# A hybrid attention layer on one core: a regrouped opening, weight copies and splits in another order, a gate that starts one step later

## The chip, the cores and the metric

One core of a Trainium2 chip runs the whole layer. The time is device microseconds of one execution, the median of three runs. "Before" is the kernel as it was, "after" the kernel with the change.

## The reference, cut to what matters

512 tokens, width 1024, float32, one layer. Group A attends over the 128 best keys that a small indexer picks for each query, group B is latent attention with low-rank queries and keys; both are causal by chunks of 64 tokens.

```python
xn = rms_norm(h, norm_gain[l])
proj = xn @ w_in[l]
(q_a, k_a, v_a, g_a, q_i, k_i, w_i, c_q, c_kv, k_rope, g_b) = jnp.split(proj, offsets, axis=-1)
q_a = rope(rms_norm(q_a), pos); k_a = rope(rms_norm(k_a), pos)      # 8 heads of 64
q_i, k_i = rope(first 32 columns), rest as it is                    # 8 index heads, one index key
o_a = indexer_sparse_attention(q_a, k_a, v_a, q_i, k_i, w_i, pos)   # top 128 keys of 512
q_b = (rms_norm(c_q) @ w_uq); kv = (rms_norm(c_kv) @ w_ukv)         # 384 and 256 wide latents
o_b = chunk_causal_attention(rope/rms q_b, rope/rms k_b, v_b, pos)
mixed = concat([o_a * silu(g_a), o_b * silu(g_b)])
h = h + mixed @ w_out[l]
```

## The kernel before, in words

Every product of two float32 operands is made of three TensorE matmuls on a high and a low half (`mm3`, line 185): high by high, high by low, low by high. The halves are made by a cast on ScalarE and a subtraction: for weights `chunk` (line 266) loads 128 rows into one of three staging tiles `wst` from SP's queue, casts on ScalarE (line 272) to `wh` and subtracts on GpSimd, or VectorE where the plan says "D", (line 275) to `wl`. Weights stand in one plan in the order of their use; `wt` makes a weight at least 8 ahead of its use, and `first` (line 231) orders a ScalarE instruction before the casts of weights that are more than so many ahead. TensorE's order is the order in which the program is written (the weaving of streams by `run`, `take`, `weave`); the other engines are put in order by a scheduler, and `after` adds an order between two instructions of one engine.

**The opening** (lines 202 to 215 and 344 to 504). SP's queue loads four 128-token tiles of x, the identity, three small gain vectors (`grow`) and the weights of the small projection (`k_rope`, `k_i`, `w_i`, 104 columns), then `q_i`'s weights. For each token tile half of the squares are summed on ScalarE and half on VectorE, added on VectorE, raised to -1/2 on GpSimd, and the tile is scaled on VectorE. Then TensorE transposes all four tiles (`x_turn`, 32 transposes); a half is two tiles, and after its second tile ScalarE writes eight high parts `xh` (line 375) and VectorE eight low parts `xl` (line 378). `small_step` (line 487) does the small projection on 256 columns of one half at a time, three matmuls for each of eight row blocks: first half 0 alone, then half 1 with one step of `q_i` after each. `stream` (line 316) interleaves the jobs of one projection: a job is a bank and its row blocks, each job starts some steps after the one before. `q_i` has three query tiles, 8/3 steps apart, and its transposes use the banks "tr". There are eight PSUM banks, named mm (3), tr (2), sc (2) and pv (1), taken in turn.

**Then** come the latent projections `c_kv` and `c_q`, the indexer, top-k passes on VectorE woven through everything, the gates `g_b` (four jobs that start together, banks pv, mm, mm, mm, line 619), the up-projections and attention B, then `g_a`, `q_a`, `k_a`, `v_a`, then attention A with the output projection woven in.

**`proj`** (line 837) handles `q_a` and `k_a`: square on ScalarE, sum on VectorE, `rope_mul` (line 412) into two tiles of the ring `tmp`, their sum at line 847, the scale, and later, in `turn`, four transposes, split, and four copies inside the core (`DUP`, line 834) by SP's queue into the two operand tiles.

**`attention`** (line 694): `qk` scores one head and query tile, adds the mask and takes the minimum on VectorE (line 707), exponentiates on ScalarE (line 709), then for each pair of tiles a reciprocal (line 726) and the normalizing product, on ScalarE (line 732) or GpSimd; `pt` transposes the probabilities in three groups and splits them (line 421); `pv` multiplies by V. `SP` holds the splits of a group, `END` the reciprocal and the products of a pair.

## Time and profile before

| | |
|---|---|
| median of three runs | 341.23 us (340.65 to 341.61) |
| the profiled execution's own time | 340.73 us |
| its span, first to last instruction | 338.9 us |
| TensorE / VectorE / ScalarE / GpSimd busy | 325.3 / 257.5 / 215.5 / 182.7 us |

Busy times of TensorE run from the start of a matmul to the end that is modelled for it; a following matmul starts earlier than that, so a short hole between two starts can hide in a busy TensorE. Idle time of an engine is put down to what ended it. A line such as L127 or L131 is that of a helper (`matmul`, `transpose`), so instructions are told apart by their tiles. Names ending in "q" are an engine's queue: SPq stands for DMA issues.

### The profile page before, as it was taken

The numbers are of one execution on the slowest core, as the hardware profiler recorded it, in microseconds if no ns is written. First come the engines' busy times: TensorE is split into PE (matmuls) and PEld (weight loads), VectorE is DVE, ScalarE is ACT, GpSimd is POOL, SyncE is SP. The second block draws the span as 40 slices with busy tenths as digits, with TensorE's granted clock in tenths as the row PEclk, the third lists the DMA queues.
The fourth block names the chain that finished last, engine by engine and source line by source line (L and its number), as shares of the span: only waits on it lengthen the run. The fifth ranks groups of instructions, "written<-read, shape, count | busy, mean of one in ns | idle before, by whom it ended". The sixth has DMA issues, their size and how long they took to land.

```text
span 338.9 us, 5472 instructions
## 1 busy us (share of the span) xinstructions
PE 325.3 (96%) x1688; PEld 272.1 (80%) x1688; DVE 257.5 (76%) x631; ACT 215.5 (64%) x530; POOL 182.7 (54%) x197
## 2 busy tenths in 40 slices
PE   2899999999999999999999999999999999999995
PEld 2778888887898988888888888888777788788884
DVE  4924679659998496778898989776997667776465
ACT  4935558582656676878877898434326988887210
POOL 1655543365799997135714579538725535647100
PEclk9999999999999999999999999999999999999999
DMA  7753344133024325014200355208877314410006
GB/s 263 202 157 93 110 118 119 60 102 93 22 82 119 96 64 155 1 34 121 69 29 1 88 140 136 74 0 201 220 171 232 102 55 140 126 63 0 2 0 248
DMA packets 28806, 34.83 MB, mean 103 GB/s; under 512 B 5341, under 2 KB 16874, under 8 KB 28778
## 3 DMA queue, kind: packets, MB, share of 16 engines
q1 hardware_dynamic: 28202, 33.57, 35.7%
q10 hardware_dynamic: 576, 0.92, 0.7%
q8 instruction: 13, 0.21, 0.3%
q14 instruction: 15, 0.12, 0.1%
HBM read 27.14 MB, written 2.10 MB: 86 GB/s over the span
## 4 chain that ended last, share of the span: by engine, by line
PE 84%; DVE 5%; ACT 3%; DMA 3%; SPq 2%; issue 1%; POOL 1%; DVEq 0%; ACTq 0%; POOLq 0%
PE mm L127 48%; PE sc L127 12%; PE pv L127 9%; PE tr L131 6%; PE tr L127 5%; PE mm L131 2%; DVE ob L946 2%; ACT xh L375 2%; DMA xin<-in_x 2%; SPq L834 1%; DMA wst<-in_w_in 1%; POOL wl L275 1%; ACT wh L272 1%; PE pv L131 1%; DVE tmp L851 0%
## 5 line engine op out<-in xcount | busy, mean ns | idle before, releaser
L275 POOL TENSOR_TENSOR wl<-wst,wh 128x512 fp32r<-128x512 f32 (+2 forms) x80 | 100.0, 1260 | 52.1 <-ACT wh L272 49.7
L272 ACT CAST wh<-wst 128x512 fp32r<-128x512 f32 (+2 forms) x89 | 51.2, 585 | 29.1 <-DMA wst<-in_w_in 22.0
L127 PE MATMUL mm<-wh,xh 128*128 128x512 f32 x120 | 50.3, 419 | 0.0
L127 PE MATMUL mm<-wl,xh 128*128 128x512 f32 x120 | 47.7, 398 | 0.8 <-POOL wl L275 0.8
L127 PE MATMUL mm<-wh,xl 128*128 128x512 f32 x120 | 47.4, 395 | 0.0
L221 POOL TENSOR_TENSOR sml<-sml,nhalf 128x4 f32<-128x4 f32 (+2 forms) x28 | 31.7, 1136 | 21.8 <-ACT sml L845 13.7
L709 ACT ACTIVATE z<-z,sml 128x256 f32<-128x256 f32 (+2 forms) x64 | 35.9, 561 | 10.4 <-DVE sml L707 9.4
L730 POOL TENSOR_SCALAR z<-z,sml 128x512 f32<-128x512 f32 (+2 forms) x32 | 18.1, 565 | 40.9 <-DVE sml L726 30.9
L127 PE MATMUL mm<-xh,wh 128*128 128x512 f32 x88 | 36.7, 418 | 0.4 <-DVE latl L470 0.4
L127 PE MATMUL mm<-xl,wh 128*128 128x512 f32 x88 | 34.8, 396 | 0.0
L127 PE MATMUL mm<-xh,wl 128*128 128x512 f32 x88 | 34.8, 395 | 0.0
L127 PEld LDWEIGHTS mm<-wh,xl 128*128 128x128 f32 x120 | 22.6, 188 | 5.3
L563 DVE MAX8 m<-acc 128x8 f32<-128x512 f32 (+2 forms) x48 | 26.4, 552 | 0.0
L127 PEld LDWEIGHTS mm<-wl,xh 128*128 128x128 f32 x120 | 22.8, 190 | 4.4 <-POOL wl L275 1.5
L564 DVE MATCH_REPLACE8 acc<-m,acc 128x512 f32<-128x512 f32 (+2 forms) x48 | 26.0, 542 | 0.0
L127 PEld LDWEIGHTS mm<-wh,xh 128*128 128x128 f32 x120 | 22.6, 189 | 3.2 <-issue 0.3
L421 DVE TENSOR_TENSOR pl<-tr,ph 128x512 fp32r<-128x512 f32 (+1 forms) x32 | 17.6, 549 | 5.3 <-ACT ph L421 5.3
L421 ACT CAST ph<-tr 128x512 fp32r<-128x512 f32 (+1 forms) x32 | 15.2, 475 | 8.8 <-PE tr L131 8.5
L707 DVE CUSTOM_DVE_ANT_0 z<-sc,wide,nqb 128x512 f32<-128x512 f32 (+3 forms) x32 | 17.3, 541 | 4.3 <-PE sc L127 4.0
L707 DVE CUSTOM_DVE_ANT_0 z<-sc,acc,nqa 128x512 f32<-128x512 f32 (+2 forms) x24 | 14.6, 610 | 7.3 <-PE sc L127 7.3
L127 PE MATMUL sc<-kl,bhl 96*128 96x512 f32 (+3 forms) x96 | 20.0, 320 | 0.0
L127 PEld LDWEIGHTS mm<-xh,wl 128*128 128x128 f32 x88 | 16.5, 188 | 4.0
(223 smaller groups left out, 863.5 us busy)
## 6 DMA issues: line engine op xcount, KB each, us to landing
wst<-in_w_in SPq DMA_DIRECT2D x48, 256.0 KB, 2.7
wst<-in_w_out SPq DMA_DIRECT2D x16, 256.0 KB, 2.9
xin<-in_x SPq DMA_DIRECT2D x4, 512.0 KB, 4.2
k_a<-tmp SPq DMA_DIRECT2D x16, 128.0 KB, 3.9
ob<-in_x SPq DMA_DIRECT2D x8, 256.0 KB, 4.4
wst<-in_w_in SPq DMA_DIRECT2D x8, 192.0 KB, 2.6
wst<-in_w_uq SPq DMA_DIRECT2D x6, 192.0 KB, 2.4
wst<-in_w_in SPq DMA_DIRECT2D x8, 128.0 KB, 2.2
```

What stands on the lines that cost most here:

```text
L127: nc.tensor.matmul(o, l, r, start=start, stop=stop)
L131: nc.tensor.transpose(o, i, idn)
L221: nc.gpsimd.tensor_tensor(dst, src, nhalf[:, :src.shape[-1]], op=OP.pow)
L272: copies.append(nc.scalar.copy(h, st))
L275: i = E(eng).tensor_tensor(l, st, f32(h), op=OP.subtract)
L375: nc.scalar.activation(h, p, AF.Copy, scale=gains[:, k:k + 1])
L421: return nc.scalar.copy(h, p), nc.vector.tensor_tensor(l, p, f32(h), op=OP.subtract)
L563: nc.vector.max(m, masks[t])
L564: dve[0] = nc.vector.match_replace(masks[t], m, masks[t], -3e38).ins
L707: m = nc.vector.tensor_tensor_reduce(z, sc[:, :n], mask(t), nq(h, t), 3e38, OP.add, OP.min, r[:, i:i + 1])
L709: e = nc.scalar.activation(z, z, AF.Exp, bias=r[:, i:i + 1], scale=-1.0, accum_out=r[:, 2 + i:3 + i])
L730: nc.gpsimd.tensor_scalar(z, z, w, 0.0, op0=OP.mult, op1=OP.add)
```

## The change

The diff with its core kept. In the opening:

- ScalarE starts with a one-element square (`wake`) and then issues the three `grow` loads itself; SP's queue has x, the identity and the small weights.
- Eleven matmuls on a zero tile (`WARM`) are first on TensorE.
- Tile 2 is squared by ScalarE alone; the two sums are added on GpSimd; tile 3 is scaled on GpSimd in two passes.
- TensorE's order is: tile 0, the gains' transpose, tiles 1 and 2, the small projection on row blocks 0 to 3 of half 0, tile 3, row blocks 4 to 7, then half 1 with steps of `q_i`. The matmuls with the low part of the small weight come last, eight of 512 columns; that part is subtracted on VectorE instead of GpSimd.
- `q_i`'s query tiles start 1.99 steps apart, each step with the low weight last (`mm3w`); banks mm, mm, pv; the transposes of two of the three use the banks "sc". `c_kv` takes mm and pv instead of pv and mm.
- `chain` fixes the order of the opening's instructions on ScalarE, VectorE and GpSimd.

Later: the four jobs of `g_b` start 0.35 steps apart, which puts the second step of the first job ahead of the fourth job's first. For `k_a` the product of `rope_mul` stays in PSUM, and two of its four `DUP` copies are issued by ScalarE. In attention A, head 1's exponentials for tiles 2 and 3 come after the products of head 0's last pair, and its passes of line 707 after the reciprocal; a head's exponential for tile 0 comes after the first split of the head before; splits come ahead of the casts of weights more than four ahead.

```diff
+    def mm3w(o, lh, ll, rh, rl, first, last):
+        matmul(o, lh, rh, first, False)
+        matmul(o, ll, rh, False, False)
+        matmul(o, lh, rl, False, last)
...
     for t in range(NT):
         nc.sync.dma_start(xin[t // 2][:, t % 2], xv[:, t])
-        if t == NT - 1:
-            for a in range(0, 8, 4):
-                ks = slice(a, a + 4)
-                nc.sync.dma_start(wst[:, ks, 0:32], wv[:, ks, 3272:3304])
-                nc.sync.dma_start(wst[:, ks, 32:104], wv[:, ks, 2560:2632])
-                nc.scalar.copy(SWH[:, ks], wst[:, ks])
-                nc.gpsimd.tensor_tensor(SWL[:, ks], wst[:, ks], f32(SWH[:, ks]), op=OP.subtract)
         if t == 1:
             nc.sync.dma_start(ident, cst[:, 768:896])
-            nc.sync.dma_start(grow[0:8], norm_gain.rearrange("(k p) -> k p", p=128))
...
+    for a in range(0, 8, 4):
+        ks = slice(a, a + 4)
+        nc.sync.dma_start(wst[:, ks, 0:32], wv[:, ks, 3272:3304])
+        nc.sync.dma_start(wst[:, ks, 32:104], wv[:, ks, 2560:2632])
...
+    zero = sb("pt2", (128, 512), name="zero")
+    nc.vector.memset(zero, 0.0)
+    warm = psum("tr")
+    for _ in range(WARM):
+        matmul(warm, zero[:, 0:128].bitcast(F32R), zero.bitcast(F32R), True, True)
+
+    wake = P.tile([128, 1], F32, name="wake")
+    wake_ = nc.scalar.activation(wake, epsc, AF.Square)
+    for d in (nc.scalar.dma_start(grow[0:8], norm_gain.rearrange("(k p) -> k p", p=128)),
+              nc.scalar.dma_start(grow[8:11], b_q_latent.rearrange("(k p) -> k p", p=128)),
+              nc.scalar.dma_start(grow[11:13], b_kv_latent.rearrange("(k p) -> k p", p=128))):
+        after(d, wake_)
...
+        if t == 2:
+            SQ[t] = nc.scalar.activation(big, xt, AF.Square, scale=D ** -0.5, accum_out=r[:, 0:1])
+            other = epsc
...
+        POW[t] = nc.gpsimd.tensor_tensor(r[:, 2:3], r[:, 0:1], other, op=OP.add), rsqrt(r[:, 3:4], r[:, 2:3])
+        SCL[t] = []
+        for xs in (xt[:, 0:512], xt[:, 512:]) if t in (0, 3) else (xt,):
+            e = nc.gpsimd if t == 3 else nc.vector
...
-            xb[hf] = [psum(b) for b in (("tr", "tr", "sc", "sc"), ("mm", "mm", "mm", "tr"))[hf]]
+            xb[hf] = [psum(b) for b in (("mm", "mm", "mm", "pv"), ("tr", "tr", "sc", "sc"))[hf]]
...
-    for t in range(NT):
-        x_turn(t)
-    sm_acc = psum("pv")
+    x_turn(0)
+    gp = psum("sc")
+    transpose(gp[:, :13], grow[:13], ident[:13, :13])
+    gains_ = nc.scalar.copy(gains, gp[:, :13])
+    x_turn(1)
+    x_turn(2)
+    sm_acc = psum("mm")
     def small_step(hf, k):
         c = slice(hf * 256, hf * 256 + 256)
-        mm3(sm_acc[:104, c], SWH[:, k], SWL[:, k], xh(k)[:, c], xl(k)[:, c], k == 0, k == 7)
+        matmul(sm_acc[:104, c], SWH[:, k], xh(k)[:, c], hf == 0 and k == 0, False)
+        matmul(sm_acc[:104, c], SWH[:, k], xl(k)[:, c], False, False)
...
+    for k in range(4):
+        small_step(0, k)
+    x_turn(3)
+    for k in range(4, 8):
+        small_step(0, k)
+    for a in range(0, 8, 4):
+        ks = slice(a, a + 4)
+        SWD.append(nc.vector.tensor_tensor(SWL[:, ks], wst[:, ks], f32(SWH[:, ks]), op=OP.subtract))
+    qi_ = stream(tok_jobs("q_i", 8, xh, xl, 512, [1, 2, 3], lambda t, a: use_qi(t, a), mm3=mm3w), 3, ("mm", "mm", "pv"), 1.99)
+    for i, ks in enumerate(((0,), (1,), (2, 3), (4, 5), (6, 7))):
+        for k in ks:
+            small_step(1, k)
+        run(take(qi_, i // 2 + 1))
+        if i == 0:
+            xa, xd = [[f[hf, k] for hf in range(2) for k in range(8)] for f in (XA, XD)]
+            chain(wake_, SQ[0], SQ[1], SQ[2], gains_, SQ[3], *xa[:2], SWA[0], *xa[2:4], SWA[1], *xa[4:8], copies[0],
+                  *xa[8:10], copies[1], *xa[10:12], copies[2], *xa[12:], copies[3], copies[4])
+            chain(TTR[0], TTR[1], *SCL[0], *SCL[1], TTR[3], *SCL[2], *xd, dsubs[0], *SWD)
+            chain(*POW[0], *POW[1], *POW[2], *POW[3], *SCL[3], *subs[:3])
...
     for k in range(8):
-        small_step(0, k)
...
+        matmul(sm_acc[:104], SWL[:, k], xh(k), False, k == 7)
...
-            p = psum("tr")
+            p = psum("tr" if t == 1 else "sc")
...
-    lkv = stream(feat_jobs("c_kv", 8, xh, xl, [(0, 128), (128, 128)], lat_kv), 2, ("pv", "mm"), 3)
+    lkv = stream(feat_jobs("c_kv", 8, xh, xl, [(0, 128), (128, 128)], lat_kv), 2, ("mm", "pv"), 3)
...
-    gb_ = stream(gate_jobs("g_b", gB), 4, ("pv", "mm", "mm", "mm"), False)
+    gb_ = stream(gate_jobs("g_b", gB), 4, ("pv", "mm", "mm", "mm"), 0.35)
...
-            if not turn and t == 3:
-                if h == 1:
+            if not turn and h == 1 and t >= 2:
+                after(e, END[0][1])
+                if t == 2:
                     after(m, END[0][0])
-                    after(e, END[0][1])
-                elif h > 1:
-                    after(m, SP[h - 2, 0][1])
+                    after(ZM[h, 3], m)
+            elif not turn and h > 1 and t == 3:
+                after(m, SP[h - 2, 0][1])
+            if not turn and h and t == 0:
+                after(e, SP[h - 1, 0][0])
...
             SP[h, b] = split(ph, pl, p[:, :n])
+            if not turn:
+                first(SP[h, b][0], KEEP_EXP)
...
-            rope_mul(q, m, a3, tab, t, 8, 64)
+            c = q if name == "q_a" else a3
+            rope_mul(c, m, a3, tab, t, 8, 64)
...
-                    DUP(a, h3[HALF[u]])
-                    DUP(b, (l3 if name == "q_a" else h3)[HALF[u]])
+                    if name == "q_a":
+                        DUP(a, h3[HALF[u]])
+                        DUP(b, l3[HALF[u]])
+                    else:
+                        DUP(a, h3[HALF[u]], nc.scalar if u else nc.sync)
+                        DUP(b, h3[HALF[u]], nc.scalar if u else nc.sync)
```

## Rows read from the trace of the kernel before

**Rows 1.** The page's part 1: busy us, share of the span, instructions of each engine.
```profile
PE 325.3 (96%) x1688; PEld 272.1 (80%) x1688; DVE 257.5 (76%) x631; ACT 215.5 (64%) x530; POOL 182.7 (54%) x197
```
**Rows 2.** Waits of TensorE from 20 us on: us in total, times, longest us.
```profile
PE mm L127 <- POOL wl L275: 0.8, 2, 0.5
PE tr L131 <- ACT z L732: 0.6, 1, 0.6
PE pv L127 <- DVE pl L421: 0.4, 1, 0.4
PE mm L127 <- DVE latl L470: 0.4, 1, 0.4
```
**Rows 3.** Timeline of the opening, SP's queue: start us, us, instruction, tiles, count.
```profile
3.10 0.83 SPq L203 DMA_DIRECT2D xin<-in_x  x2
...
16.10 18.68 SPq L268 DMA_DIRECT2D wst<-in_w_in  x13
```
**Rows 4.** The same timeline, ScalarE: the fourth square and two first casts.
```profile
9.13 0.63 ACT L348 ACTIVATE tmp<-xin 128x512 f32<-128x512 f32 x1 [1.00 <-DMA xin<-in_x]
...
9.77 1.19 ACT L375 ACTIVATE xh<-tr,gains 128x256 fp32r<-128x256 f32 x3
...
14.01 0.89 ACT L375 ACTIVATE xh<-mm,gains 128x256 fp32r<-128x256 f32 x2
```
**Rows 5.** The same timeline, VectorE: the scaling of the fourth tile.
```profile
11.41 1.69 DVE L355 TENSOR_SCALAR xin<-xin,sml 128x512 f32<-128x512 f32 x2
```
**Rows 6.** The same timeline, TensorE.
```profile
7.67 1.06 PE L131 MATMUL sc<-ident,xin 128*128 128x128 f32 x4
...
10.47 0.88 PE L131 MATMUL mm<-ident,xin 128*128 128x128 f32 x6
...
13.56 0.36 PE L127 MATMUL pv<-xh,swh 128*104 128x256 f32 x1
...
16.82 0.39 PE L127 MATMUL mm<-wh,xh 128*128 128x512 f32 x1
...
19.55 0.50 PE L127 MATMUL mm<-wl,xh 128*128 128x512 f32 x1 [0.23 <-POOL wl L275]
```
**Rows 7.** The same timeline, GpSimd: the first low halves of weights.
```profile
14.77 2.56 POOL L275 TENSOR_TENSOR wl<-wst,wh 128x512 fp32r<-128x512 f32 x2
...
18.20 1.29 POOL L275 TENSOR_TENSOR wl<-wst,wh 128x512 fp32r<-128x512 f32 x1 [0.87 <-ACT wh L272]
```
**Rows 8.** Timeline from 76 to 79 us, TensorE, and below it VectorE.
```profile
76.82 0.39 PE L127 MATMUL mm<-xl,wh 128*128 128x512 f32 x1
77.05 0.40 PE L127 MATMUL mm<-xh,wl 128*128 128x512 f32 x1
77.81 0.50 PE L127 MATMUL mm<-xh,wh 128*128 128x512 f32 x1 [0.37 <-DVE latl L470]
...
77.02 0.74 DVE L470 SCALAR_TENSOR_TENSOR latl<-mm,gains,lath 128x512 fp32r<-128x512 f32 x1
```
**Rows 9.** Timeline from 228 to 245 us: SP's queue, and below it TensorE.
```profile
233.31 2.94 SPq L834 DMA_DIRECT2D k_a<-tmp  x4
236.35 0.55 SPq L268 DMA_DIRECT2D wst<-in_w_in  x1
...
242.26 3.08 SPq L834 DMA_DIRECT2D qz<-q_a  x2
...
240.98 0.39 PE L127 MATMUL mm<-wh,xh 128*128 128x512 f32 x1
241.91 0.51 PE L127 MATMUL mm<-wl,xh 128*128 128x512 f32 x1 [0.54 <-POOL wl L275]
```
**Rows 10.** Timelines in attention A: ScalarE from 261, VectorE from 286 us.
```profile
262.54 0.62 ACT L709 ACTIVATE z<-z,sml 128x384 f32<-128x384 f32 x1 [0.56 <-DVE sml L707]
...
263.16 0.49 ACT L732 ACTIVATE z<-z,sml 128x256 f32<-128x256 f32 x1
...
288.20 0.58 ACT L421 CAST ph<-mm 128x512 fp32r<-128x512 f32 x1
...
289.31 0.69 DVE L421 TENSOR_TENSOR pl<-mm,ph 128x512 fp32r<-128x512 f32 x1
```

More of the change, by code (lines that the diff above doesn't have):

```diff
@@ L55 @@
 LAG_KA = 10500
+KEEP_SMALL = 1
 KEEP_QI = 5
@@ L62 @@
 KEEP_UP = 4
+WARM = 11
 TK = (2, 5, 5, 13, 12, 6)
@@ L229, in after, with chain @@
             mybir.DependencyClass.NoSync, mybir.DependencyReason.DATA), reason="order")
+    def chain(*ins):
+        for v, u in zip(ins[1:], ins):
+            after(v, u)
+    zero = sb("pt2", (128, 512), name="zero")
[9 more added lines that the diff above has]
+        after(d, wake_)
     def first(ins, m):
@@ L294, in layer, with tok_jobs @@
         weight(n, *{'oa1': ('PPPD', 'AD'), 'oz1': ('PPPD',)}.get(n, "P"))
-    def tok_jobs(name, nk, lh, ll, n, tiles, use, c=0):
+    def tok_jobs(name, nk, lh, ll, n, tiles, use, c=0, mm3=mm3):
         def job(t):
@@ L346, in layer @@
         r = small(4)
[L347 to L361 removed]
+        if t == 2:
+            SQ[t] = nc.scalar.activation(big, xt, AF.Square, scale=D ** -0.5, accum_out=r[:, 0:1])
+            other = epsc
+        else:
+            sq = tmp(), tmp()
+            SQ[t] = nc.scalar.activation(sq[0], xt[:, 0:512], AF.Square, scale=D ** -0.5, accum_out=r[:, 0:1])
+            TTR[t] = nc.vector.tensor_tensor_reduce(sq[1], xt[:, 512:], xt[:, 512:], 1.0 / D, EPS, OP.mult, OP.add, r[:, 1:2])
+            other = r[:, 1:2]
+        POW[t] = nc.gpsimd.tensor_tensor(r[:, 2:3], r[:, 0:1], other, op=OP.add), rsqrt(r[:, 3:4], r[:, 2:3])
+        SCL[t] = []
+        for xs in (xt[:, 0:512], xt[:, 512:]) if t in (0, 3) else (xt,):
+            e = nc.gpsimd if t == 3 else nc.vector
+            if t == 3:
+                SCL[t].append(e.tensor_scalar(xs, xs, r[:, 3:4], 0.0, op0=OP.mult, op1=OP.add))
+            else:
+                SCL[t].append(e.tensor_scalar(xs, xs, r[:, 3:4], None, op0=OP.mult))
+    xb, XA, XD = {}, {}, {}
     def x_turn(t):
@@ L429, in use_small @@
         st = tmp()
-        nc.scalar.copy(st[:104], a[:104])
+        first(nc.scalar.copy(st[:104], a[:104]), KEEP_SMALL)
         def turn():
```

55 lines of the change are left out of this document (21 added, 34 removed).

## Prediction, made before the change was run

> **What bounds the kernel now.** I read the page first: TensorE is busy for 325.3 of 338.9 us, every other engine for at most 76% [rows 1]. Next to look at is therefore where TensorE is *not* fed. The waits of TensorE from 20 us on are only four kinds [rows 2]: a low weight half from GpSimd (0.8 us, two times), a normalized tile from ScalarE, a low half of the probabilities and one of a latent from VectorE. Between these TensorE runs start to start without a hole, so the time is: the moment at which this dense stream begins, plus a fixed amount of matmul time, plus those few holes, plus a tail after the last matmul that the change doesn't touch. Only the first and the holes can move. Third, the timeline of the opening shows what the stream waits for at its beginning [rows 3 to 7]; fourth, the timelines of the holes [rows 8 to 10]. The profiled execution took 340.73 us, 1.8 us more than its span and 0.50 less than the median of the three runs (341.23). I make the sum against 340.73 and add the 0.50 at the end.
>
> A 512-column matmul costs 0.23 us, the distance of two starts that nothing delays (76.82 and 77.05) [rows 8]; a step of three costs 0.70 us. From 13.56 to 16.82 stand 27 matmuls of 256 columns, 0.12 us each [rows 6].
>
> **The opening, step by step.** *Before:* ScalarE can't begin its casts of the transposed x (`xh`) until it has squared the fourth token tile, which starts at 9.13 when that tile lands; the first cast starts at 9.77 [rows 4]. VectorE scales the fourth tile from 11.41 on, in two passes that share 1.69 us with other work [rows 5]. TensorE stands idle for much of the time up to 13.56, since all 32 transposes come before the first matmul; from there it is dense but for the wait at 19.55, where the third `q_i` low half arrives [rows 6, 7]: 0.4 us by starts, 0.23 shown as idle.
>
> *(a) Earlier x.* Three small loads leave SP's queue ahead of tiles three and four, whose issue at 3.10 [rows 3] comes about 1.0 us sooner. They move to ScalarE's queue, where nothing else runs before the first square. I take 0.8 us for the landing of tile four, between 0 (the transfers, not the issue, set it) and 1.0. The first cast then starts at about 9.0. The tile's scaling goes to GpSimd, the low split of the small weight from GpSimd to VectorE behind the x splits; the fourth scaling on GpSimd, two 512-column passes, is bounded by two of its subtractions (2.56 us) [rows 7], and the transposes that need it come only after the matmuls on the first half, so it is covered.
>
> *(b) What runs when.* In the new hand-written order ScalarE does, from the first cast to the second half's first cast, the same list as before: eight casts, two of the small weight, one of `q_i`. That took 14.01 - 9.77 = 4.24 us [rows 4]. So the second half's first cast starts near 13.2, its VectorE split ends near 14.0, and there the dense stream begins. By then TensorE has already done the small projection on the first half: 16 matmuls of 256 columns, 16 x 0.12 = 1.9 us, in the hole that stood before 13.56. The eight matmuls with the low weight are now 512 wide: no columns are saved. Stream start 14.0 against 13.56 costs 0.4; the third `q_i` low half comes after 12 casts instead of 16 and GpSimd no longer has the two small-weight splits in front of it, so three subtractions from 13.2 on make it ready near 13.2 + 3 x 1.3 = 17.1 against 18.20 + 1.3 = 19.5 [rows 7], and the 0.4 at 19.55 mostly goes (0.3). Sum: 1.9 - 0.4 + 0.3 = **1.8 us**. If tile four does not land earlier it is 1.0; if the stream starts as early as before it is 2.3. These are its bounds, with one more: the staging ring. The fourth weight load is issued at 16.10 [rows 3], when the first GpSimd subtraction has ended (14.77 plus 1.3) [rows 7]; in the new order that subtraction starts near 13.2, so the load goes at 14.5. With its query tiles 1.99 instead of 2.67 steps apart the stream asks for new weights more slowly. I cost the feed at nothing; without that cover a late weight costs one subtraction, 1.3 us.
>
> *(c) The clock.* The granted clock of this chip has two levels, 1.2 and 2.4 GHz; the column shows 1.00 for the opening, but transposes follow each other every 0.21 to 0.23 us from 7.67 and six of them take 0.88 us from 10.47 [rows 6], so the clock rose to 2.4 GHz about there, after nothing but transposes. The eleven zero matmuls take at most 11 x 0.46 = 5.1 us at half rate and begin once VectorE has cleared their operand, one 512-column pass of 0.7 us [rows 10] at the very start; so they end by 7 at the latest, when the first tile's transposes run now (the second four of its eight start at 7.67 [rows 6]). They cost nothing, bounded by the 0.3 us by which they could overrun, and bring the 0.11 spacing forward to the transposes of tiles one and two.
>
> The Trainium skill speaks against this: "TensorE: Matmul & The Clock Gate", section Part 4: PE-mode transpose, says that transposes do not count as TensorE being busy, so that the full rate does not engage for them. By that rule the warmed clock would fall again during the transposes; by the trace, where it rose after transposes alone, it would stay. By the trace the sum is as above; by that rule it would be rival 1 below.
>
> **The fourth gate.** At 77.05 TensorE has started its last matmul before the fourth gate's first; that one starts at 77.81 because its bank is still read by the latent split that runs on VectorE from 77.02 for 0.74 us [rows 8]. The hole is 0.76 - 0.23 = 0.53, and 0.1 follows while the pipeline refills. Putting one step (0.70) of the first gate in between covers it: **0.6 us**, bounds 0 (the split is reached later, or weight two is not there) and 0.65. Next late there is the second gate weight, asked for 0.70 us sooner; no wait on it is seen [rows 2].
>
> **k_a.** The low half used at 241.91 was late by 241.91 - 240.98 - 0.23 = 0.7, and 0.1 of refill follows: it comes from a load that SP issued only at 236.35, behind four copies of `k_a` that held the queue from 233.31 for 2.94 us [rows 9]. Two of the four go to ScalarE's queue, so the load is issued about 1.5 us sooner and the hole goes: **0.7 us**, bounds 0 and 0.8. ScalarE pays two issues a tile, 0.74 us each by the same row, eight in all. The product written into PSUM instead of the query tile changes no count; it holds the projection's bank for one VectorE operation longer, which I cost at 0, bounded by that operation, 0.7.
>
> **Attention A.** At 263.16 ScalarE normalizes the tile TensorE waits for, after an exponential of the next head (262.54, 0.62 us) [rows 10]; the new order puts all such exponentials of head one, and the VectorE passes before its reciprocal, behind. At 288.20 ScalarE makes the first split's high half behind the exponential of the next head, and its low half runs at 289.31, which is the 0.4 us wait of `pv` [rows 2, 10]. The two waits are 0.6 and 0.4 [rows 2], by starts 0.2 to 0.5 more each (a matmul counts as busy for 0.4, but the next one could start after 0.23). I take about half, **0.8 us**, since the score bank of the next head is freed later by the same edit: bounds 0 and 1.8. Weight casts are pushed behind the splits, each by one split, 0.58 us [rows 10]; loads run several weights ahead, so 0.
>
> **Small moves with a price near nothing.** The second `c_kv` tile and the third `q_i` tile now share a bank, the `q_i` transposes use the score banks: a wait of 0 to 0.5 at one place each; no row shows it, and I take 0.
>
> **Sum:** 1.8 + 0.6 + 0.7 + 0.8 = 3.9; 340.73 - 3.9 = 336.8, and with the 0.50, 337.3.
>
> **Rivals.**
> 1. *The opening gives nothing.* The clock falls again during the transposes (the rule cited above), or the gain loads hold ScalarE's queue before its squares. At the 0.22 spacing the last two transpose groups and the 8 matmuls between take about 2 us more, the stream starts at 16 and the 1.8 is gone: 339.1. For it: ScalarE's work in the opening is one chain. Against: the clock rose at about 10.3 [rows 6]. 0.15.
> 2. *Holes move instead of going.* The same transfers, bank or VectorE pass ends the wait a little later, at 77, 241, 262 and 290 together: only the opening stays, 341.23 - 1.8 = 339.4. For it: VectorE is nearly full there. 0.13.
> 3. *Slower: ScalarE blocked by its copies.* A copy that can't be issued waits in its queue, with weight casts behind it. SP shows such a hold: two `qz` copies from 242.26 take 3.08 us, 1.6 more than two issues at 0.74 [rows 9]. On ScalarE a tile's pair would then cost 1.5 + 1.6 = 3.1; less the 1.5 us by which the load now comes sooner, 1.6 for each tile held. Without k_a's 0.7 the other terms give 3.2, so it decides from two tiles held on; with three the time is 341.23 - 3.2 + 3 x 1.6 = 342.8. Against: ScalarE has long idle stretches there, and issues are spread over 20 us. 0.06.
> 4. *No change that counts:* 341.2, when 1 and 2 come together. 0.06.
>
> **How the numbers follow.** The forecast has 0.60; its own bounds run from 1.0 to 2.3 + 0.65 + 0.8 + 1.8 = 5.55 less, 335.7 to 340.2. About 0.3% (1.0 us) is what a measurement of this kernel can tell from no change. Forecast and rivals 1 and 2 are faster by more than that (0.88); rival 4 and a sliver of the others are the same (0.07), rival 3 slower (0.05). The range for 8 in 10 reaches from the lower of these bounds past rivals 1 and 2: 335.7 to 339.9.
>
> **What would show it.** Right: first cast near 9.0, first second-half split by 14, transposes 0.11 apart before 9, no wait of TensorE on `latl` near 76 or on `wl` near 238, the last matmul 3.9 us sooner than now. Wrong: transposes at 0.21, ScalarE's first square long after the first tile lands, waits of ScalarE's queue ahead of weight casts near 235 to 250, new waits of TensorE on a bank near 38 or 45.

## The result, and the profile after

The kernel after takes 339.30 us (median of five executions, 339.12 to 340.48) against 341.23 (also the median of five): 0.995 of the time before, interval 0.9932 to 0.9968. That is 1.9 us of the 3.9 that were forecast. Its profiled execution took 339.3 us with a span of 337.5; span against span the gain is 1.4 us (338.9 before). Two later executions, one of the fourth gate alone (462.7 us) and the profiled one of the kernel after on another chip (362.5 us), ran at a low clock throughout and stand in no median and no ratio.

Part 1 of the page of the kernel after, to be read against [rows 1]. TensorE's busy time is 2.8 us higher, since the eleven zero matmuls are counted (5.1 us), and the span is shorter:

```profile
PE 328.1 (97%) x1691; PEld 273.8 (81%) x1691; DVE 259.0 (77%) x627; ACT 216.2 (64%) x531; POOL 184.5 (55%) x201
```

The waits of TensorE from 20 us on, the view of [rows 2] (us in total, times, longest us):

```profile
PE mm L130 <- POOL mal L828: 0.4, 1, 0.4
PE mm L130 <- DVE tmp L905: 0.4, 1, 0.4
PE sc L134 <- DVE tmp L571: 0.3, 1, 0.3
PE sc L130 <- DVE sml L758: 0.2, 1, 0.2
PE pv L130 <- DVE pl L449: 0.2, 1, 0.2
```

The waits of before on `wl`, `z` and `latl` are gone, as forecast. In their place stand three that were not there before: on `mal` (low half of A's gated output), on the add of `k_a` (L905) and on the rope add of a `q_i` tile (L571). A small one, on `sml` (L758), is new as well.

How much each place gave or took can be read by counting TensorE's instructions back from the last one in both traces and comparing the starts of the same instruction. The gain accumulates from top to bottom; the last column is what each place adds:

| place (us in the kernel before) | gain so far | this place |
|---|---|---|
| end of the opening, 38 | 0.57 | +0.57 |
| third `q_i` tile's transposes, 41 | 0.01 | -0.55 |
| fourth gate, 78 | 0.79 | +0.57, and 0.10 each before and behind it |
| `k_a`: low weight half, 242 | 1.45 | +0.65 |
| `k_a`: bank held for the add, 244 | 0.93 | -0.52 |
| first normalized tile of A, 264 | 1.38 | +0.80, after -0.36 at 254 and 262 |
| first splits of A, 290 to 291 | 1.90 | +0.77, after -0.26 |
| small waits up to 300, `mal` at 312 | 1.12 | -0.32, and -0.45 at `mal` |
| last matmul to the end of the span | 1.43 | +0.31 |

The opening of the kernel after, from its timeline (start us, us, engine, line, operation, tiles, count, idle before); the lines answer [rows 3 to 7]:

```profile
2.11 0.92 SPq L212 DMA_DIRECT2D xin<-in_x  x2
...
6.75 0.88 PE L134 MATMUL mm<-ident,xin 128*128 128x128 f32 x6 [0.24 <-DVE xin L387]
...
9.22 0.63 ACT L377 ACTIVATE tmp<-xin 128x512 f32<-128x512 f32 x1 [0.17 <-DMA xin<-in_x]
...
9.85 0.82 ACT L403 ACTIVATE xh<-mm,gains 128x256 fp32r<-128x256 f32 x2
...
11.15 0.66 PE L134 MATMUL tr<-ident,xin 128*128 128x128 f32 x4 [1.71 <-DVE xin L387]
...
14.09 0.89 ACT L403 ACTIVATE xh<-tr,gains 128x256 fp32r<-128x256 f32 x2
14.32 3.79 POOL L298 TENSOR_TENSOR wl<-wst,wh 128x512 fp32r<-128x512 f32 x3 [1.35 <-ACT wh L295]
15.01 0.88 DVE L406 SCALAR_TENSOR_TENSOR xl<-tr,gains,xh 128x256 fp32r<-128x256 f32 x2 [0.31 <-ACT xh L403]
15.63 5.52 SPq L291 DMA_DIRECT2D wst<-in_w_in  x4
15.75 0.39 PE L130 MATMUL mm<-wh,xh 128*128 128x512 f32 x1
```

Tiles three and four are issued 1 us earlier (2.11), and the first six transposes take 0.88 us, so TensorE's clock is already up. But the square of tile four starts at 9.22, when that tile lands, against 9.13 [rows 4]: nothing came sooner. The window tables, the kernel before first, show what the DMA engines did (columns: window, its length, busy us and counts of PE, PEld, DVE, ACT, POOL, granted clock, share of the 16 DMA engines' time, GB/s):

```profile
2.50:4.50 2.00, 0.00 (x0) 0.00 (x0) 0.47 (x1) 0.47 (x1) 0.00 (x0) 1.00 1.03 410
4.50:6.50 2.00, 0.25 (x1) 0.18 (x1) 1.55 (x6) 1.15 (x5) 0.57 (x1) 1.00 1.20 350
```

```profile
2.50:4.50 2.00, 2.00 (x6) 1.61 (x5) 0.27 (x1) 0.27 (x1) 0.00 (x0) 1.00 1.00 395
4.50:6.50 2.00, 2.00 (x5) 0.99 (x4) 1.34 (x5) 1.18 (x4) 0.82 (x3) 1.00 1.02 257
6.50:7.50 1.00, 0.76 (x8) 0.75 (x8) 0.59 (x2) 0.00 (x0) 0.92 (x2) 1.00 1.05 410
7.50:9.00 1.50, 1.15 (x11) 0.89 (x9) 0.75 (x1) 1.16 (x3) 0.00 (x1) 1.00 1.08 318
```

In both kernels the engines move some 400 GB/s from 2.5 to 4.5 us; at that rate a tile of 0.5 MB takes 1.3 us (an estimate). Tile three was asked for at 3.10 in the kernel before, when tile two was still on its way (ScalarE's square of it starts at 5.34, when it lands). Asking sooner made it wait longer, not land sooner. In the kernel after the share reads 1.02 from 4.5 to 6.5 at only 257 GB/s, but that window isn't even: from 5.5 to 6.0 the share is 0.36, so the engines had some slack there, and what holds tile three in that stretch isn't shown. More traces say the same of the landing: VectorE's pass over tile four, which starts as the tile lands, begins at 8.8 to 10.1 us in the six traces with the old opening and at 9.0 to 10.7 in the ten with the new one and all of x on SP's queue.

### The profile page after: what moved, and what is told of

Its sections match the earlier page's. It is cut to its first block, busy times and chain, and to the rows that moved or that the text cites. A ratio compares the mean times of both kernels' runs of the same rounds, so it can differ in the third digit from the quotient of the medians.

```text
span 337.5 us, 5484 instructions
## 1 busy us (share of the span) xinstructions
PE 328.1 (97%) x1691; PEld 273.8 (81%) x1691; DVE 259.0 (77%) x627; ACT 216.2 (64%) x531; POOL 184.5 (55%) x201
## 4 chain that ended last, share of the span: by engine, by line
PE 74%; DVE 10%; DMA 5%; issue 4%; ACT 4%; POOL 2%; SPq 1%; DVEq 0%; POOLq 0%
PE mm L130 40%; PE sc L130 11%; PE pv L130 10%; PE tr L134 5%; PE tr L130 5%; DMA wst<-in_w_in 3%; DMA xin<-in_x 2%; DVE ob L1008 2%; PE mm L134 2%; DVE acc L617 1%; DVE z L758 1%; DVE m L616 1%; ACT xh L403 1%; POOL sml L226 1%; POOL wl L298 1%
## 5 line engine op out<-in xcount | busy, mean ns | idle before, releaser
L130 PE MATMUL mm<-wh,xh 128*128 128x512 f32 x112 | 47.1, 420 | 0.4 <-DVE tmp L905 0.4
L130 PE MATMUL mm<-wl,xh 128*128 128x512 f32 x112 | 44.5, 397 | 0.0
L130 PE MATMUL mm<-wh,xl 128*128 128x512 f32 x112 | 44.3, 395 | 0.0
L784 POOL TENSOR_SCALAR z<-z,sml 128x512 f32<-128x512 f32 (+2 forms) x32 | 17.9, 560 | 42.1 <-DVE sml L780 31.4
L226 POOL TENSOR_TENSOR sml<-sml,nhalf 128x4 f32<-128x4 f32 (+2 forms) x28 | 32.5, 1163 | 14.9 <-ACT sml L903 13.7
L130 PEld LDWEIGHTS mm<-wh,xl 128*128 128x128 f32 x112 | 21.1, 188 | 4.8
L130 PEld LDWEIGHTS mm<-wl,xh 128*128 128x128 f32 x112 | 21.2, 189 | 3.5 <-POOL wl L298 0.3
L130 PEld LDWEIGHTS mm<-wh,xh 128*128 128x128 f32 x112 | 21.1, 189 | 3.6 <-issue 0.8
L449 DVE TENSOR_TENSOR pl<-tr,ph 128x512 fp32r<-128x512 f32 (+1 forms) x32 | 17.6, 550 | 5.7 <-ACT ph L449 5.5
L449 ACT CAST ph<-tr 128x512 fp32r<-128x512 f32 (+1 forms) x32 | 15.1, 473 | 9.1 <-PE tr L134 8.8
L758 DVE CUSTOM_DVE_ANT_0 z<-sc,wide,nqb 128x512 f32<-128x512 f32 (+3 forms) x32 | 17.3, 542 | 4.2 <-PE sc L130 4.0
L130 PEld LDWEIGHTS sc<-kl,bhl 96*128 96x128 f32 x96 | 16.6, 189 | 3.0
```

Of the source, the lines that this page charges most:

```text
L130: nc.tensor.matmul(o, l, r, start=start, stop=stop)
L226: return nc.gpsimd.tensor_tensor(dst, src, nhalf[:, :src.shape[-1]], op=OP.pow)
L449: return nc.scalar.copy(h, p), nc.vector.tensor_tensor(l, p, f32(h), op=OP.subtract)
L758: m = nc.vector.tensor_tensor_reduce(z, sc[:, :n], mask(t), nq(h, t), 3e38, OP.add, OP.min, r[:, i:i + 1])
L784: nc.gpsimd.tensor_scalar(z, z, w, 0.0, op0=OP.mult, op1=OP.add)
```

## The experiments

The runs below were made on other chips than the comparison above; each ratio is against the kernel before on the same chip (medians 341.3, 341.3 and 341.7 us there). The four single edits to the kernel after under "The three new waits" ran once each, on one more chip, and are read by their traces alone. Differences of one place are read from matched starts, as in the table.

### Each part alone

**The opening alone** (the other edits undone).

> The kernel after with only its new opening: fourth gate, k_a and attention A are as in the kernel before. Theory (new waits): by the starts on TensorE, counted from the last matmul, the opening has brought 0.56 us at 38 us and loses 0.55 at 41.1 us, where the transposes of the third q_i tile wait for VectorE. The opening alone is then worth 0.0 us, with bounds 0.0 and 0.5: 340.7 to 341.3 against 341.2, and the wait near 41 us stands in its profile. Rival (the opening's gain is there and is eaten by the later edits): 340.2 or less, and the first half of the trace is over 1 us ahead of the kernel before. Rival (the forecast of 1.8 us): 339.4.

Measured: ratio 0.9991 (0.9974 to 1.0007). The wait at 41 us is there:

```profile
PE sc L134 <- DVE tmp L571: 0.3, 1, 0.3
```

and the trace shows something else, TensorE's clock (windows, as above; it is the column that reads 0.50):

```profile
10.00:12.00 2.00, 0.70 (x6) 0.70 (x7) 1.58 (x5) 2.00 (x7) 1.82 (x4) 1.00 1.05 333
12.60:14.00 1.40, 1.40 (x9) 1.40 (x8) 1.11 (x4) 1.40 (x5) 0.51 (x1) 0.50 0.81 274
14.00:16.00 2.00, 2.00 (x12) 2.00 (x11) 1.68 (x5) 2.00 (x6) 1.52 (x2) 0.50 0.21 46
```

From 12.6 to 16.0 us the granted clock is 1.2 GHz in place of 2.4. It had been up since 5.8; before the fall TensorE stood idle for 2 us, waiting for tile three. So part of this ratio is a fall of the clock, taken up below. The theory's 0.0 us is within the interval, the rival's 1 us is not.

**The fourth gate alone.**

```
-    gb_ = stream(gate_jobs("g_b", gB), 4, ("pv", "mm", "mm", "mm"), False)
+    gb_ = stream(gate_jobs("g_b", gB), 4, ("pv", "mm", "mm", "mm"), 0.35)
```

> The kernel before with only the fourth gate set a step later (0.35 instead of False). Theory: the wait of 0.4 us for the latent's last low part near 76 us goes and nothing takes its place: 0.55 us faster, 340.7 against 341.2. Rival (holes move): the same as before within 0.2 us, with a new wait of the gate streams or of the index scores behind 78 us.

Measured: 0.9974 (0.9958 to 0.9991). The wait on `latl` is gone and no new one follows; by matched starts 0.53 at 78 us and 0.10 right behind it, 0.63 together. The theory holds.

**k_a alone** (both of its edits, as in the diff).

> The kernel before with only the edits to k_a: half of the copies are issued by ScalarE, and the rope product stays in the projection's PSUM bank. Theory (each part has its own price): the copies give 0.63 us at 242 us, the bank that is held until the add costs 0.5 us at about 244 to 245 us: 0.1 us faster, 341.1, with a wait of TensorE's mm bank for the add on VectorE in its profile. Rival (the bank's wait comes only from the phase that the other edits set): no such wait, 340.6. Rival (ScalarE blocked by its own issues): slower than before.

Measured: 0.9995 (0.9982 to 1.0009). By matched starts +0.65 at 242 us and -0.67 at 245, the second for the add of `k_a`:

```profile
PE mm L127 <- DVE tmp L849: 0.5, 1, 0.5
```

The bank's wait does not depend on the other edits. The gain is given back in full.

**Attention A alone** (its hunks of the diff).

> The kernel before with only attention A's edits (order of its exponentials, and the first splits ahead of the weight casts). Theory: the start of the attention gains 0.8 us at 264 to 270 us and some 0.6 at 290, and loses 0.45 at the last pv (311 us), where GpSimd's low part of ma comes late, and some 0.3 to 0.6 in small waits: 0.3 to 0.5 us faster, 340.7 to 340.9. Rival (the splits before the casts cost nothing): 0.8 or more faster, 340.4 or less, without the wait at 311. Rival (holes move): 341.2.

Measured: 0.9995 (0.9976 to 1.0015). By matched starts from 261 us on: -0.35 at 262, +0.86 at 264, -0.22 up to 270, +0.78 at 290 and 291, -0.17 and +0.24 up to 296, -0.34 from 298 to 300, -0.54 at 312, together +0.26. The waits in its trace:

```profile
PE mm L127 <- POOL mal L777: 0.4, 1, 0.4
PE sc L127 <- DVE sml L707: 0.4, 1, 0.4
```

The places are as the theory had them, with the wait at 311 us; the sum is a little under its 0.3, and 0.26 us is within what the ratio can't tell from nothing.

**Everything but the opening, beside the kernel after on one chip.**

> The kernel before, opening and all, with the three later edits (fourth gate, k_a, attention A). Theory: the parts add up: 0.57 for the gate, 0 to 0.1 for k_a and 0.36 for attention A, 1.0 us in all, 0.997 of the time before. What the kernel after has beyond that beside it is the opening's: 0.3 to 0.9 us, of the 1.8 forecast. Rival (the opening is worth nothing): the same time as the kernel after.

> The kernel after itself, on the chip of the three runs beside it. Theory: 0.995 of the time before, as at first, with waits of about 0.5 us at 41 and 0.6 at 311 us, and one of 0.5 us or more either at 241.9 us (the weight's low part) or at 243.4 us (the bank held for k_a's add), whichever is later in this execution. If the wait at 241.9 is back here, its place in the first trace was a matter of one load's landing.

Measured: 0.9975 (0.9962 to 0.9987) for the three later edits, 0.9948 (0.9931 to 0.9966) for the kernel after. (Which wait the kernel after had on this chip, at 242 or at 243 us, is not known. In five traces with its `k_a` edits and the new opening, on the other chips and on this one, the wait is for the add, at 243 to 246 us; in one, that with the transposes' own banks, it is for the low half, at 242.) The later edits are worth 0.9 us, give or take 0.4, and the opening the other 0.9, give or take 0.7. That is more than the table leaves for the opening: 0.57 - 0.55, or 0.3 with the shorter tail. The trace of the kernel with the old opening suggests where that comes from. It has a wait at 27 us that the profile of the kernel before doesn't show:

```profile
20.33 6.81 SPq L268 DMA_DIRECT2D wst<-in_w_in  x4
...
24.81 1.90 ACT L272 CAST wh<-wst 128x512 fp32r<-128x512 f32 x3 [3.86 <-DMA wst<-in_w_in]
25.51 2.52 POOL L275 TENSOR_TENSOR wl<-wst,wh 128x512 fp32r<-128x512 f32 x2 [3.19 <-ACT wh L272]
...
26.84 0.50 PE L127 MATMUL mm<-wl,xh 128*128 128x512 f32 x1 [0.86 <-POOL wl L275]
```

The load issued at 20.33 took 4.5 us to land here, in the profile before 2.9 (20.15 to 23.00). All five traces of experiments with the old opening have this wait (0.6 to 1.1 us by starts, at 26 to 27 us); no trace with the new one has it at that place. There the load of the same weight, the sixth, is issued some 2 us sooner, at 17.9 to 19.7 us in eleven traces against 19.9 to 21.4 in the six with the old opening, so that even a slow landing is in time. Which edit of the opening frees its staging tile sooner wasn't tried; the spacing of the query tiles isn't it, since the trace with even spacing (below) has the load at 17.9 and no wait.

### The three new waits

**41 us.** Two runs, one for the bank and one for the spacing of the query tiles:

```
-            p = psum("tr" if t == 1 else "sc")
+            p = psum("tr")
```

> The kernel after with all three transposes of q_i in the banks for transposes, as in the kernel before, in place of score banks for the second and third. Theory: the wait of 0.47 us at 41.1 us is for the tile's own rope add on VectorE, so the bank has nothing to do with it: the wait stays within 0.1 us, and up to 0.3 us of new bank waits come on top. Rival: the score bank does it (VectorE's instructions on the second tile's bank push the third's add back): the wait falls under 0.2.

```
-    qi_ = stream(tok_jobs("q_i", ...), 3, ("mm", "mm", "pv"), 1.99)
+    qi_ = stream(tok_jobs("q_i", ...), 3, ("mm", "mm", "pv"), True)
```

> The kernel after with the three index queries spaced evenly (8/3 steps) as in the kernel before, in place of two steps. Theory: the tiles end 2.1 us apart again instead of 1.4, VectorE keeps up, and the wait of 0.47 us at 41.1 us goes; the first weights are wanted sooner, so a wait for a weight's low part of 0.4 us or more comes back between 16 and 21 us: net 0.1 faster to 0.3 slower. Rival: the wait at 41.1 us is set by VectorE's start of its work on the third tile whatever the spacing, and stays.

With the transposes' own banks the wait changes its place and its name: TensorE waits 0.3 (0.41 by starts, at 40.1) for VectorE's `qi` split, which frees the bank. That is neither theory nor rival as told: the wait for the add went, and the bank's came in its place. With even spacing the wait is gone, 0.50 us by starts at 41, and the early part loses only 0.15 at 20 us, for a low half: the weights came nearly in time. Waits of TensorE with even spacing, and with them, from the timeline of the kernel after, what VectorE did before 41 us:

```profile
PE mm L130 <- POOL mal L828: 0.4, 1, 0.4
PE mm L130 <- DVE tmp L905: 0.4, 1, 0.4
PE pv L130 <- DVE pl L449: 0.2, 1, 0.2
PE sc L130 <- DVE sml L758: 0.2, 1, 0.2
```

```profile
39.09 0.42 DVE L443 TENSOR_TENSOR tmp<-pv,cs 128x256 f32<-128x256 f32 x1
...
39.46 0.69 DVE L449 TENSOR_TENSOR kil<-tr,kih 128x512 fp32r<-128x512 f32 x1
40.07 0.42 DVE L446 TENSOR_TENSOR pv<-pv,cs 128x256 f32<-128x256 f32 x1
40.53 0.42 DVE L571 TENSOR_TENSOR tmp<-pv,tmp 128x256 f32<-128x256 f32 x1
...
41.10 0.52 PE L134 MATMUL sc<-ident,tmp 128*128 128x128 f32 x3 [0.31 <-DVE tmp L571]
```

The three tiles end closer together, so VectorE has the splits of the first `q_i` tile and of `k_i` (L449) to do amid the rope of the third, and the third's add (L571) comes at 40.53. With even spacing it is done at 38.85 to 39.27. The spacing is the cause; the bank would be one as well, since the old banks wait too.

**243 us.** Product back in SBUF, copies kept; then the copies alone in the kernel before (only the second hunk):

```
-            c = q if name == "q_a" else a3
-            rope_mul(c, m, a3, tab, t, 8, 64)
+            rope_mul(q, m, a3, tab, t, 8, 64)
```

```
-                    DUP(a, h3[HALF[u]])
-                    DUP(b, (l3 if name == "q_a" else h3)[HALF[u]])
...
+                        DUP(a, h3[HALF[u]], nc.scalar if u else nc.sync)
+                        DUP(b, h3[HALF[u]], nc.scalar if u else nc.sync)
```

> The kernel after, with k_a's rope product back in its SBUF tile (the copies on ScalarE stay). Theory: TensorE's wait of 0.54 us at 243.4 us for the add on VectorE goes, since the bank comes free one VectorE instruction earlier; 0.5 us less from there to the end, and the gain of 0.6 at 242 us stays. Rival: the bank comes free too late either way (the wait was there, hidden, behind the 0.7 us wait for the weight's low part): the wait stays at 0.3 or more.

> The kernel before with half of k_a's copies issued by ScalarE and nothing else; the rope product stays in SBUF. Theory (GpSimd's order decides: its clear of qz stays ahead of the weight's low part unless the product leaves SBUF): the wait of 0.7 us at 241.9 us stays at 0.5 or more and the time is that of the kernel before within 0.3 us. Rival (the copies alone free SyncE for the weight load, the step of the prediction): the wait goes, 0.6 us faster.

In the first, the wait for the add went (0.54 by starts), and one of 1.4 us (1.54 by starts) for the low weight half came back: neither theory nor rival. The second is slower than the kernel before: 1.0047 (1.0027 to 1.0067). Its waits, and GpSimd and TensorE there:

```profile
PE mm L127 <- POOL wl L275: 1.9, 3, 1.0
```

```profile
241.40 0.52 POOL L918 MEMSET qz<- 64x512 f32 x1 [1.59 <-DVE kl L866]
...
242.00 2.51 POOL L275 TENSOR_TENSOR wl<-wst,wh 128x512 fp32r<-128x512 f32 x2
...
243.33 0.50 PE L127 MATMUL mm<-wl,xh 128*128 128x512 f32 x1 [1.03 <-POOL wl L275]
```

The copies do bring the weight load forward (issued 235.66 against 236.35, while TensorE is 0.9 us later there). But GpSimd's clear of `qz` stands ahead of the low half in its order, and idles 1.59 us for VectorE's split of `kl`; the low half waits behind it. In the kernel after, where the product is in PSUM, the same clear comes behind two more low halves:

```profile
241.01 1.29 POOL L298 TENSOR_TENSOR wl<-wst,wh 128x512 fp32r<-128x512 f32 x1 [0.61 <-ACT wh L295]
...
243.97 0.52 POOL L976 MEMSET qz<- 64x512 f32 x1
```

So the step "two copies fewer in SP's queue, so the hole goes" is refuted as told: copies alone take 0.5 us at this place. By these traces the gain at 242 came with GpSimd's changed order, a side effect of the PSUM edit, and the same edit costs the 0.5 at 243. The product in PSUM without the copies wasn't run, so what the copies add to it isn't known. The rest of the 1.6 us by which this kernel is slower the trace doesn't show.

**311 us.** Without the edit that puts the first splits ahead of the weight casts:

```
-            if not turn:
-                first(SP[h, b][0], KEEP_EXP)
```

> The kernel after without the one edit that puts attention A's first splits ahead of the weight casts; the order of the exponentials stays. Theory: the wait of 0.6 us at 310.7 us (GpSimd's low part of the last ma, queued behind the low part of the weight whose cast came late) shrinks to 0.1; the gain of 0.8 us at 264 us, which is the exponentials' order, stays; the gain of 0.6 at 290 us, where a split waited behind a cast, goes: net 0.1 slower to 0.1 faster. Rival A: the gain of 0.8 at 264 us is the splits' and goes too: 0.8 slower. Rival B: the gain at 290 us is the exponentials' and stays: 0.5 faster.

The wait on `mal` went (+0.53), the gain at 264 stayed, the one at 290 went (-0.84 by 291): 0.27 slower together, the theory's reading, a little worse than its 0.1. What happens at 306 to 311 us in the kernel after:

```profile
306.50 0.57 ACT L449 CAST ph<-tr 128x512 fp32r<-128x512 f32 x1
306.96 0.59 ACT L449 CAST ph<-mm 128x512 fp32r<-128x512 f32 x1
307.44 0.63 ACT L295 CAST wh<-wst 128x512 fp32r<-128x512 f32 x1
...
308.15 1.30 POOL L298 TENSOR_TENSOR wl<-wst,wh 128x512 fp32r<-128x512 f32 x1 [0.49 <-ACT wh L295]
309.40 1.28 POOL L828 TENSOR_TENSOR mal<-tmp,mah 128x512 fp32r<-128x512 f32 x1
```

Head 6's splits go ahead of a weight cast; GpSimd, which makes that weight's low half and then `mal`, idles 0.49 us for the cast, and TensorE waits for `mal`.

**All three mended.** First with the product back in SBUF and GpSimd's clears ordered behind the last root of `k_a`, and only head 7's splits let behind the casts (besides the even spacing):

```
-            rsqrt(r[:, 8:16], r[:, 0:8])
+            KPOW.append(rsqrt(r[:, 8:16], r[:, 0:8]))
...
-        nc.gpsimd.memset(f32(QZ[u][HALF[1 - u]]), 0.0)
+        after(nc.gpsimd.memset(f32(QZ[u][HALF[1 - u]]), 0.0), KPOW[-1])
...
-            if not turn:
+            if not turn and h < n_ - 1:
                 first(SP[h, b][0], KEEP_EXP)
```

> The kernel after with the new waits mended: index queries spaced evenly again, k_a's rope product back in SBUF while GpSimd's clears of qz are ordered behind the last k_a reciprocal root, and the first split of the last head no longer ahead of the weight casts. Theory (each new wait has its own cause): the waits of 0.47 us at 41, 0.54 at 243 and 0.60 at 311 us go: 1.5 us faster than the kernel after, 337.8 against 339.3 (337.5 to 338.2). Rival (the waits only move on): 338.7 or more, with waits of like size at other places.

Measured: 0.9964 (0.9951 to 0.9977). By matched starts +0.5 at 41 and +0.54 at 243, but -0.58 at 242 (the low half again: its weight's cast waited for the load until 239.46, 1.1 us later than in the kernel after) and nothing at 311, where it is head 6's splits that matter. For `k_a`, then, each mend has brought back the other wait. Second, with even spacing, `k_a` as in the kernel after, and:

```
-            if not turn:
+            if not turn and h < 6:
                 first(SP[h, b][0], KEEP_EXP)
```

> The kernel after with the index queries spaced evenly again and the first splits put ahead of the weight casts for heads 0 to 5 only; k_a as in the kernel after. Theory: the waits at 41 us (0.47) and 311 us (0.60) go, the gain at 290 us stays: 0.9 to 1.0 us less than the kernel after beside it, from the same opening. Rival (the casts that are let ahead of head 6's splits make those late): a wait of 0.3 us or more behind 307 us, and 0.5 us less only.

Measured: 0.9926 (0.9909 to 0.9943), 338.91 us in the median, beside 0.9948 for the kernel after on this chip. The waits left are three:

```profile
PE mm L130 <- DVE tmp L905: 0.4, 1, 0.4
PE pv L130 <- DVE pl L449: 0.2, 1, 0.2
PE sc L130 <- DVE sml L758: 0.2, 1, 0.2
```

By matched starts against the kernel after, +0.50 at 41 and +0.55 at 311, less 0.1 of small waits between them: the 0.9 to 1.0 us expected. This version is faster than the kernel before, and its six executions (338.56 to 339.18) all lie below the five of the kernel after beside it (339.30 to 340.15), though the two intervals overlap.

### The opening

**Both queues for x.**

```
-        nc.sync.dma_start(xin[t // 2][:, t % 2], xv[:, t])
+        (nc.scalar if t % 2 else nc.sync).dma_start(xin[t // 2][:, t % 2], xv[:, t])
```

> The kernel after with the x tiles issued in turn by SyncE and ScalarE, so that all four are issued by about 1.8 us. Theory (the transfers set the landing, not the issue): the fourth tile lands within 0.2 us of the 9.2 us of the kernel after, and the time is the same within 0.3 us. Rival (the issue sets it, the step of the prediction): the fourth tile lands 0.5 us or more earlier, at 8.7 or before, and the dense stream with it: 338.8.

Measured: 0.9975 (0.9963 to 0.9988). ScalarE in its timeline:

```profile
0.73 0.89 ACTq L212 DMA_DIRECT2D xin<-in_x  x2
...
6.06 0.63 ACT L377 ACTIVATE tmp<-xin 128x512 f32<-128x512 f32 x1 [2.91 <-DMA xin<-in_x]
...
8.96 1.06 ACT L373 ACTIVATE big<-xin 128x1024 f32<-128x1024 f32 x1 [1.56 <-DMA xin<-in_x]
```

All four tiles were issued by 1.7 us. The pass that waits for the last of them starts at 8.96, 0.26 us sooner than in the kernel after; the first came later (5.5 against 4.2), and TensorE's transposes began at 8.3 in place of 6.7. The issue doesn't set the landing, as the theory says; that the time would stay the same was wrong (0.8 us more, by the ratios, whose intervals just touch, and by starts, where all of it is there at 20 us).

**No zero matmuls** (`WARM = 0`), and **the idle stretch filled** (seven more matmuls on zeros between the transposes of tiles two and three, in the first mended kernel):

```
 x_turn(1)
+gap = psum("sc")
+for _ in range(7):
+    matmul(gap, zero[:, 0:128].bitcast(F32R), zero.bitcast(F32R), True, True)
 x_turn(2)
```

> The kernel after without its eleven matmuls on a tile of zeros ahead of the first transposes. Theory (the clock at the first transposes is worth little, since the second half waits for its tiles anyway): transposes 0.21 us apart at 6.7 us as in the kernel before; the first half's casts start 0.7 us later, and ScalarE's chain of casts carries that to the dense stream: 0.4 to 0.9 us slower than the kernel after (339.7 to 340.2 where the kernel after has 339.3). Rival A (tile four's landing hides it): no difference, 339.3. Rival B (the clock then falls or stays low up to 14 us or more): 1.2 us or more slower, 340.5.

> The kernel with the new waits mended, and seven more matmuls on zeros in TensorE's idle 1.7 us between the second and the third x tile (9.4 to 11.1 us). Theory (the idle stretch lets the clock fall to its lower level for 3.4 us in some executions, at a price of about 1 us each): no execution has a mean clock under 0.997, the slowest executions go, and the median is 0 to 0.4 us below the mended kernel without the fill. Rival (the fall comes from the transposes and not from the idle stretch): as many executions with a mean clock of 0.996 or less as without the fill, and the same median. Rival (the fill is in the way when tile three lands early): 0.2 us or more slower.

Without the zero matmuls the ratio is 0.9977 (0.9959 to 0.9995) against 0.995 of the kernel after on the other two chips, about 0.9 us more (the intervals overlap a little), and the clock is recorded at its upper level only from 16.6 us on; the transposes run 0.21 apart. With the fill it is 0.9964 (0.9947 to 0.9980), the same as without it (0.9964). What the fill changed is the clock, read as the mean granted clock of each execution; in the four traces of the new opening that read 0.995 or less it goes with a stretch of 3.4 us at half rate between 11 and 16 us, as in the trace above:

| kernel | executions | at 0.995 or less | median of these | of the others |
|---|---|---|---|---|
| after, first chip | 5 | 2 | 340.3 | 339.3 |
| opening alone | 12 | 5 | 341.9 | 340.7 |
| x on two queues | 10 | 7 | 340.3 | 340.1 |
| mended, first version | 8 | 5 | 339.9 | 340.3 |
| mended, second version | 6 | 3 | 339.1 | 338.9 |
| no zero matmuls | 10 | 0 | | 340.7 |
| mended, filled | 9 | 0 | | 340.0 |

In the kernel after on the third chip it read so low in none of five executions; in the 82 of the kernel before that stood beside the experiments, in none; in the other kernels with the old opening, in two (of the eight with the copies alone). By the medians the fall costs between nothing and 1.2 us. That this depends on whether it ends before the dense stream (in the first mended kernel it lasted to 14.95, in the opening alone to 16.0) is argued, not shown. With the fill it came in none of nine executions, without it in five of eight; the median did not gain. One thing goes with the fall in the nine traces of the new opening that have the zero matmuls and no fill: in the four with a fall the clock had gone up at 4.5 to 5.8 us, in the five without at 5.9 to 6.9. TensorE's idle stretch ahead of tile three doesn't tell them apart (1.4 to 2.0 us in the four, 1.6 to 2.0 in four of the five; with x on two queues it lies elsewhere).

## Why the prediction went wrong, point by point

- **Direction and range** held: faster, and 339.3 lies within 335.7 to 339.9. The size was half.
- **(a) Earlier x, 0.8 us: wrong.** The earlier issue was read as an earlier landing. Tile four landed 0.1 later. The case "the transfers, not the issue, set it" stood there as the bound 0; the profile before, with tile three issued 2.2 us ahead of tile two's landing and 410 GB/s between, would have said it was the likely one.
- **(b) The dense stream at 14.0: wrong, 15.55.** Of the 1.55, 0.85 is (a): the first cast came at 9.85, not 9.0. The casts from there to the second half's first took 4.24 us, as forecast. The rest is that VectorE's first second-half split waits for a pair of casts (14.09 + 0.89) and starts at 15.01; I had it end 0.8 us after the first cast began. The 1.9 us of the small projection did move into idle time, and the wait at 19.55 went. By profile 0.57 remains of 1.8 (1.9 - 2.0 + 0.4 makes 0.3; the rest lies in gaps of under 0.12 us that I didn't follow). Over executions the opening brought some 0.9; it also removes a wait at 26 to 27 us that the one profile of the kernel before happened not to have, which is the likely difference. (By its own terms, 1.9 and 0.3, the upper bound of 2.3 should read 2.2, which changes no conclusion.)
- **(c) The clock:** the zero matmuls worked as forecast, transposes 0.11 apart from 6.75, and without them some 0.9 us is lost. Rival 1's fall of the clock came too, in about half of the executions, at 0 to 1.2 us each. It came behind up to 2 us of idleness and behind transposes, and in no execution when the idleness was filled; the transposes alone are not shown to be the cause. "TensorE: Matmul & The Clock Gate", section Part 4: PE-mode transpose, of the Trainium skill has transposes not count as TensorE being busy, so that the full rate would not engage for them. The traces of these fp32 transposes don't agree: in all six with the old opening the clock is recorded at its upper level, at 9.9 to 14.8 us, before the first matmul that isn't a transpose (13.3 to 15.3 us), and the transposes go from 0.21 to 0.11 us apart there. The 10.3 us that the prediction read was among the early ones.
- **The fourth gate, 0.6: right,** 0.63 alone, by starts.
- **k_a, 0.7: wrong, 0.1 in the profile, 0 alone.** The failed step is the product in PSUM "which I cost at 0, bounded by that operation, 0.7": in eight of the nine traces that had it TensorE waits 0.3 to 0.9 us for the add, and in the ninth the low half comes late instead. And the gain was put down to SP's queue; by the traces it came with GpSimd's order. Rival 3 (ScalarE blocked by its copies) did not happen in the kernel after: its copies there take 0.60 to 0.69 us each and no cast waits long for them.
- **Attention A, 0.8: mis-sized, 0.26 alone.** The two waits gave all of their starts (0.80 and 0.77); what I had halved for caution wasn't the trouble. "Weight casts are pushed behind the splits ... so 0" failed: 0.5 at 311 us, through GpSimd's queue. Small new waits at 262 and 298 took most of the rest.
- **Small moves at 0 to 0.5, taken as 0: the upper bound came true** at 41 us (0.55), by the spacing of two steps.
- **Rival 2 (holes move)** described the later half best: of 2.9 us that holes gave from 78 us on, by the table 0.65 + 0.80 + 0.77 + 0.67, the new waits at 243, 254 to 262 and 311 took back 1.3 us, and the small ones in the two rows with 290 and 300 another 0.6.

## What to carry to other kernels

Before counting on an earlier issue, look whether the transfer ahead of it has landed by then: here tile three was asked for 2.2 us before tile two landed, and asking 1 us sooner moved no landing forward. A term costed at nothing that has a bound of 0.5 us is not nothing on an engine that has no slack: three such terms, each on the queue of another engine (VectorE's twice, GpSimd's once), took back 1.5 us, and each had its bound or its size written beside it. Compare an edit against more than one trace of the kernel before where loads are late by chance, and look at every engine's order after an edit, since a buffer that moves can change the order of an engine that the edit never names.

## What the runs showed of the hardware

- The time from issue to landing of one 0.25 MB load, at the same place behind the same opening, was 2.9 us in one trace and 4.0 to 4.5 in five; a wait of 0 to 1.1 us of TensorE hung on it.
- Asked for 0.9 to 1.0 us sooner behind two tiles that were still in transfer, two tiles of x of 0.5 MB each landed no sooner (tile four's pass at 8.8 to 10.1 us in six traces, at 9.0 to 10.7 in ten).
- Eleven matmuls on zeros from 1.45 us on brought the granted clock to its upper level at 4.5 to 6.9 us; in about half of the executions it fell again for 3.4 us, with an idle stretch of 1.4 to 2.0 us ahead of the fall. With seven matmuls on zeros in that stretch it didn't fall in nine executions.
- fp32 transposes alone brought the clock to its upper level in six traces of six, at 9.9 to 14.8 us, those of x having started at 6.7 to 6.8; with the new opening and no zero matmuls it came only at 16.6, behind other matmuls too.
- The stretch from the start of the last matmul to the end of the span is 3.97 to 4.00 us in all traces with the new opening and 4.28 to 4.42 in those with the old one. Nothing of the change touches it; the cause is open.
